# A slot of its own for the fourth weight chunk of an output projection

## The chip, the cores and the metric

The kernel runs on one core of a Trainium2 chip. The metric is the device time of one execution, in microseconds (us); lower is better. The engines are called PE (TensorE, matmuls; PEld are its weight loads), DVE (VectorE), ACT (ScalarE), POOL (GpSimd) and SP (SyncE, which here only issues DMAs). Each engine works off its own list of instructions in order.

## What is computed

One layer of an encoder over 1024 prompt tokens and 256 sample tokens, width 1024, all in float32. Shortened:

```
n  = rmsnorm(h);  z = n @ w_in
oa = diff_attention(...)          # 4 heads, two softmax maps each
ob = gqa_attention(...)           # 8 query heads, 2 kv heads
h  = h + concat(oa, ob) @ w_out   # the output projection
h  = h + relu(rmsnorm(h) @ w_ff1)**2 @ w_ff2
h  = h + sigmoid(rmsnorm(h) @ w_gate) * (p @ w_proj)
y  = rmsnorm(h)
```

## The kernel before

Float32 products are made from three matmuls of split operands: a high part (the value rounded to a shorter format, by an ACT copy) and a low part (the value less the high part, by a subtraction), multiplied as high x high, high x low and low x high. So every weight is loaded raw, split by ACT and POOL or DVE, and then used.

The stages are: the input projections, attention, the feed-forward layer, the gate. Attention is laid out in rounds; each round has a few score matmuls, softmax pieces, transposes (`tr`), splits of the transposed weights (`ph`, `pl`) and value matmuls (`av`). Between the pieces of a round the program weaves other matmul work from one generator, `side_work`: first the rest of the query and key projections (`qk_rest`, tiles `psa`, whose results `zl` are scaled by the row `R`), then the output projection in two passes, each over four of the eight 128-row chunks of `w_out`. The first pass takes chunks 0, 1, 4 and 5 (`first` is true), the second 2, 3, 6 and 7. A pass goes over the ten 128-token tiles in the order `TORD`; for each it loads the attention result `mt` (512 KB, from DRAM, where attention stores it as `md`), makes two groups of 12 matmuls into `pso` (4 chunks x 3 products, 512 columns each), and adds them to the residual row `h_sb` on DVE (L973). In the first pass each `mt` load is followed on SP by the load of a token row from `x` (L929).

The memory on the right-hand side of a partition is first used by the pools of the projections (`xh` and `xl`, the split inputs, `R`, the weight and result buffers). `open_out_proj` (L874) closes them and opens, over the same bytes, seven slots H0 to H6 of 10,240 bytes and nine slots W0 to W8 of 4,096. Two further slots, Q0 and Q1, lie on the left. A slot holds one tile at a time: whoever takes it next waits until all readers of the tile before are done.

What the change touches is the loading of the first pass's weights in `out_proj`, L931 to L939:

- chunk 0 is loaded into Q1 by `qk_rest` (L869), long before;
- chunks 1 and 4 are loaded by `opw_dma` without a tag: their halves land in the unused last quarters of the residual tiles H1 to H4 (`h_sb<-in_w_out` in the profile);
- the fourth, chunk 5, is loaded into Q1 again (L938), after the split of chunk 0; `wor<-in_w_out` in the profile is Q1's loads, chunk 0's and chunk 5's;
- `opw_split` (L905) splits each chunk in two halves: two ACT copies (L914) and two POOL subtractions (L915). `Y` sets how many rounds pass between the splits.

`load_mt` (L922) gives the `mt` tiles W6, W7 and W8 in turn, so the first `mt` lies in W6, the second in W7 and the third in W8.

The code gives each instruction its dependencies; the order of each engine's list, SP's among them, is drawn up when the program is built, from when each instruction is expected to be ready. It is therefore not the order of the code: chunk 0's load, in the code at the end of `qk_rest`, is issued at 213.1 us, and chunk 5's, in the code ahead of the first `mt` load, behind the third.

Of the kernel before, what the change touches and what calls it, by code (L numbers as in the profile page):

```python
# [41 lines left out]
def f(ap):  # L42
    return ap.bitcast(F32)
# [3 lines left out]
def encoder_kernel(ctx: ExitStack, tc: tile.TileContext, x, xT, pT, w_in, w_out, w_ff1, w_ff2, w_gate, w_proj,  # L47
# [168 lines left out]
    def slot(tag, shape, dt, name):  # L216
        return slot_pool[tag].tile(shape, dt, tag=tag, name=name, bufs=1)
# [63 lines left out]
    def mm_gen(ps, pairs, step=6):  # L281
        n = len(pairs)
        for i, (a, b) in enumerate(pairs):
            PE.matmul(ps, a, b, start=i == 0, stop=i == n - 1)  # L284
            if i % step == step - 1:
                yield step * ps.free_size() * 0.422
        if n % step:
            yield (n % step) * ps.free_size() * 0.422
# [583 lines left out]
    op_state = {}  # L872
# [11 lines left out]
    def h_row(t):  # L884
        j, half = divmod(TORD.index(t), 2)
        return op_state["h"][j][:, half * D:half * D + D]
# [6 lines left out]
    def opw_dma(ch, tag=None):  # L893
        if tag:
            t = slot(tag, [P, D], F32, "wor")
            raws = [t[:, i * 512:i * 512 + 512] for i in range(2)]
        else:

            n = next(raw_n) % 2
            raws = [op_state["h"][2 * n + i + RO][:, 2 * D:] for i in range(2)]  # L900
        for i in range(2):
            dma(raws[i], w_out[ch * P:(ch + 1) * P, i * 512:i * 512 + 512])
        return raws

    def opw_split(raws):  # L905
        n = next(ow_n) % 5
        if n < 2:
            w = slot32(f"H{5 + n}", [P, 2, D], F32R, "ow")
            a, b = w[:, 0], w[:, 1]
        else:  # L910
            a, b = (slot(f"W{2 * n - 4 + i}", [P, D], F32R, "ow")[:] for i in range(2))
        for i, raw in enumerate(raws):
            c = slice(i * 512, i * 512 + 512)
            S.activation(a[:, c], raw, AF.Copy)  # L914
            G.tensor_tensor(b[:, c], raw, f(a[:, c]), op=ALU.subtract)  # L915
        return a, b

    def out_proj(chs, ws, ahead, banks, first):

        mts = {}  # L920

        def load_mt(it):  # L922
            t = TORD[it]
            mt = mts[it] = slot(("W6", "W7", "W8")[it % 3 if first or it < 6 else it % 2], [P, 4, 2, P], F32R, "mt")
            d = dma(f(mt[:]), md[0 if first else 1][:, :, :, t * P:(t + 1) * P])
            if first:
                with tc.issue_after(d.ins):
                    for t_ in TORD[it + XA if it else 0:it + 1 + XA]:
                        dma(h_row(t_), x[t_ * P:(t_ + 1) * P])  # L929

        if first:  # L931
            raws = [op_state.pop("w0"), opw_dma(chs[1]), opw_dma(chs[2])]
            for n in range(4):
                for _ in range(Y[n > 0]):
                    yield 0.0
                ws.append(opw_split(raws.pop(0)))
                if n == 0:
                    raws.append(opw_dma(chs[3], "Q1"))  # L938
                    load_mt(0)  # L939
        else:  # L940
            raws = []
            for n, ch in enumerate(chs):
                if n >= len(ws):
                    raws.append(opw_dma(ch))
                    if len(raws) == 2:
                        yield 0.0
                        yield 0.0
                        ws.append(opw_split(raws.pop(0)))
            while raws:
                ws.append(opw_split(raws.pop(0)))  # L950
        nb = 0
        for it, t in enumerate(TORD):
            while any((ch, t // 2 * 256) not in md_done for ch in chs):
                yield 0.0
            if it not in mts:
                load_mt(it)
            mt = mts.pop(it)
            if it == 0:
                for _ in range(Y[2]):
                    yield 0.0  # L960
            for n0 in range(0, D, 512):
                ps = banks[nb % len(banks)]("pso")
                nb += 1
                pr = []
                for i in range(4):
                    mh, ml = (mt[:, i, v, :] for v in range(2))
                    a, b = (w[:, n0:n0 + 512] for w in ws[i])
                    pr += [(mh, a), (mh, b), (ml, a)]
                yield from mm_gen(ps, pr, 3)

                def evac(ps=ps, t=t, n0=n0):
                    h = h_row(t)[:, n0:n0 + 512]
                    V.tensor_tensor(h, ps, h, op=ALU.add)  # L973

                deferred.append(evac)
                yield 0.0
            if not first:
                op_done.append(t)
            if ahead and it in (2, 5):
                ahead.pop(0)()  # L980
# [4 lines left out]
    def side_work():  # L985
        yield from qk_rest()
        flush()
        open_out_proj()
        chs2 = (2, 3, 6, 7)
        ahead = []  # L990
        for ch in chs2[:2]:
            box = []
            ahead.append(lambda ch=ch: w_next.append(opw_split(opw_dma(ch))))
        yield from out_proj((0, 1, 4, 5), [], ahead, [pj], True)
        yield from out_proj(chs2, w_next, None, banks2, False)
# [884 lines left out]
```

## Time and profile before

| | |
|---|---|
| median of 3 runs | 1682.07 us (1681.45 to 1683.6) |
| profiled execution | 1681.64 us |
| its span, first to last instruction | 1679.9 us |
| mean granted TensorE clock | 0.996 |
| DMA traffic | 309.22 MB, mean 184 GB/s |
| DMA in 420 to 440 us, 440 to 460 us | 239 and 299 GB/s |

The profile is of one execution. A busy share counts the time in which an engine executes; idle time is put down to what ended it. A timeline row gives the start, the length, the engine, the line in the code, the operation, and the tile written and those read, without buffer numbers; in square brackets stands how long the engine had been idle before it and what released it. A window row gives the busy time of each engine in a stretch, then the TensorE clock granted (1.00 is full), the mean busy share of the DMA engines, and what they moved. SPq is SP's DMA queue: a row there is the issue of a transfer, whose landing is told apart. Attention ends, and the feed-forward layer begins, at some 750 us; the first output projection's matmuls begin at 444.9 us.

### The profile page before, as it was taken

To read this page: it belongs to the slowest core of one execution; us is meant where nothing else is said; L and a number is where in the kernel's file an instruction comes from. 1 tells how busy PE (TensorE), PEld (TensorE's weight loads), DVE (VectorE), ACT (ScalarE), POOL (GpSimd) and SP (SyncE) were. 2 spreads that over 40 slices of the span, in tenths; PEclk is the share of its full clock that TensorE was granted. 3 is DMA by queue.
4 is the path that set the end of the run, shared out by engine and by line. 5 is a ranking of instruction groups with operands and counts; after the bars stand their busy time and mean duration, and the time that the engine had idled before them with its cause. 6 is when DMAs were issued, how large, how long until landed. Compare 5 with 4: busy or idle time off the path is not lost. (4 is left out here: it accounts for less than half of the span.)

```text
span 1679.9 us, 27290 instructions
## 1 busy us (share of the span) xinstructions
PE 1639.0 (98%) x9777; PEld 1469.5 (87%) x9777; DVE 1202.9 (72%) x2130; ACT 879.3 (52%) x1716; POOL 664.2 (40%) x697
## 2 busy tenths in 40 slices
PE   8999999999899999999999999999999999999996
PEld 8999888888788888888999999998888888888885
DVE  7778588777788888668766666666664866855876
ACT  8543377776766667665333333333433435745533
POOL 1223455555653445333656656620433400003342
PEclk9999999999999999999999999999999999999998
DMA  9666843432954434295434443339676459980453
GB/s 330 222 221 240 246 143 112 133 109 93 271 170 129 144 87 135 95 327 192 160 118 135 148 137 132 132 137 387 233 234 196 160 187 354 337 287 13 164 205 107
DMA packets 205964, 309.22 MB, mean 184 GB/s; under 512 B 14714, under 2 KB 124932, under 8 KB 205828
## 3 DMA queue, kind: packets, MB, share of 16 engines
q1 hardware_dynamic: 203940, 301.96, 54.5%
q0 software_dynamic: 1600, 5.24, 1.1%
q8 instruction: 77, 1.26, 0.3%
q14 instruction: 59, 0.48, 0.1%
q10 hardware_dynamic: 288, 0.27, 0.0%
HBM read 200.45 MB, written 101.72 MB: 180 GB/s over the span
## 5 line engine op out<-in xcount | busy, mean ns | idle before, releaser
L671 PE MATMUL sc<-kt,qt 128*128 128x512 f32 (+1 forms) x576 | 156.4, 391 | 6.6 <-ACT p L696 4.4
L736 DVE TENSOR_TENSOR pl<-tr,ph 128x512 fp32r<-128x512 f32 x204 | 137.9, 684 | 33.7 <-ACT ph L731 32.1
L731 ACT ACTIVATE ph<-tr 128x512 fp32r<-128x512 f32 x204 | 119.8, 595 | 57.0 <-PE tr L725 50.3
L1411 DVE TENSOR_TENSOR ao<-ar,ao 128x1280 fp32r<-128x1280 f32 x56 | 96.1, 1716 | 72.0 <-ACT ao L1409 71.9
L1409 ACT ACTIVATE ao<-ar 128x1280 fp32r<-128x1280 f32 x56 | 71.0, 1270 | 128.4 <-PE f__14937 L176 31.6
L284 PE MATMUL pso<-ow,mt 128*128 128x512 f32 x480 | 120.0, 396 | 4.1 <-ACT ow L914 1.7
L725 PE MATMUL tr<-ident,p 128*128 128x128 f32 x768 | 116.0, 274 | 6.1 <-DVE pl L736 5.4
L671 PEld LDWEIGHTS sc<-kt,qt 128*128 128x128 f32 x576 | 98.9, 189 | 24.7 <-ACT p L696 5.9
L725 PEld LDWEIGHTS tr<-ident,p 128*128 128x128 f32 x768 | 91.7, 141 | 22.8 <-DVE pl L736 9.0
L284 PEld LDWEIGHTS pso<-ow,mt 128*128 128x128 f32 x480 | 87.6, 188 | 22.5 <-DVE osq L776 2.0
L1125 POOL TENSOR_SCALAR w1r<-w1r,gmlp 128x256 f32<-128x256 f32 x112 | 80.2, 733 | 67.8 <-DMA w1r<-in_w_ff 67.8
L749 PE MATMUL av<-ph,vt 128*128 128x256 f32 x544 | 101.7, 288 | 1.2 <-ACT ph L731 0.7
L710 POOL TENSOR_SCALAR p<-p,rl 128x1024 f32<-128x1024 f32 x64 | 76.1, 1190 | 50.8 <-DVE rl L708 44.5
L1198 ACT ACTIVATE w<-w1s 128x512 fp32r<-128x512 f32 x56 | 35.2, 629 | 114.7 <-POOL w1s L1205 54.9
L1696 PE MATMUL psg<-gbo,gao 128*128 128x512 f32 (+1 forms) x387 | 91.0, 385 | 0.0
L688 DVE TENSOR_REDUCE mm<-sc 128x1 f32<-128x1024 f32 (+1 forms) x80 | 84.2, 1055 | 8.9 <-PE sc L671 8.4
L749 PE MATMUL av<-pl,vt 128*128 128x256 f32 x408 | 89.1, 300 | 0.0
L1801 POOL TENSOR_TENSOR ra<-ra 128x512 f32<-128x512 f32 x5 | 7.1, 1429 | 204.9 <-DVE gao L1542 204.9
L749 PEld LDWEIGHTS av<-ph,vt 128*128 128x128 f32 x544 | 81.8, 188 | 6.5 <-ACT ph L731 0.9
L696 ACT ACTIVATE p<-sc,mm 128x1024 f32<-128x1024 f32 x64 | 71.3, 1115 | 25.4 <-DVE mm L688 16.7
L1696 PEld LDWEIGHTS psg<-gbo,gao 128*128 128x128 f32 x387 | 70.9, 188 | 14.7
L684 DVE CUSTOM_DVE_ANT_0 p<-sc,dist 128x1024 f32<-128x1024 f32 x64 | 77.6, 1218 | 7.8 <-PE sc L671 3.8
(1548 smaller groups left out, 4816.1 us busy)
## 6 DMA issues: line engine op xcount, KB each, us to landing
ar<-ad SPq DMA_DIRECT2D x56, 640.0 KB, 5.2
w2r<-in_w_ff SPq DMA_DIRECT2D x56, 512.0 KB, 5.1
qt<-qd SPq DMA_DIRECT2D x160, 128.0 KB, 2.9
ad<-q SPq DMA_DIRECT2D x64, 320.0 KB, 2.9
ad<-qs SPq DMA_DIRECT2D x48, 320.0 KB, 2.2
w1r<-in_w_ff SPq DMA_DIRECT2D x28, 512.0 KB, 4.2
md<-ml SPq DMA_DIRECT2D x40, 256.0 KB, 2.5
mt<-md SPq DMA_DIRECT2D x20, 512.0 KB, 5.9
```

What stands on the lines that cost most here:

```text
L284: PE.matmul(ps, a, b, start=i == 0, stop=i == n - 1)
L671: PE.matmul(ps[:, h0:h0 + n], shared["q"][:, cc, v, i * P:(i + 1) * P], kt[:, s0 + h0:s0 + h0 + n], start=v == 0, stop=v == 1)
L684: V.tensor_tensor_reduce(out=p[:, :sn], in0=ps[:, :sn], in1=dst_t[:, off:off + sn], scale=SLOPES[idx], scalar=3.0e38, op0=ALU.add, op1=ALU ...
L688: V.tensor_reduce(out=st["m", i][:, 0:1], in_=ps[:, :sn], axis=AX.X, op=ALU.max, negate=True)
L710: G.tensor_scalar(p[:, :sn], p[:, :sn], rl[:, 0:1], 1.0, op0=ALU.mult, op1=ALU.mult)
L725: PE.transpose(t[:, jj, i * P:(i + 1) * P], st["ws"][i][:, j * P:(j + 1) * P], ident)
L731: S.activation(ph, st["tr", j2], AF.Copy)
L736: V.tensor_tensor(pl, st["tr", j2], f(st["ph", j2][:]), op=ALU.subtract)
L749: PE.matmul(st["av"][:, :256], x_, y_, start=j2 == 0 and n == 0, stop=j2 == nj - 1 and n == len(pr) - 1)
L1125: G.tensor_scalar(raw[:, k], raw[:, k], gmlp[:, 4 * kh + k:4 * kh + k + 1], 1.0, op0=ALU.mult, op1=ALU.mult)
L1411: V.tensor_tensor(ao[:, 1], a, f(ao[:, 0]), op=ALU.subtract)
L1696: ends[:] = [PE.matmul(ps, a, w, start=n == 0, stop=n == len(pr) - 1)]
```

## The change

The fourth chunk's load moves ahead of the first split, directly behind the loads of the second and third chunk, and its raw weights land in slot W8 in place of Q1. The load in the loop goes.

```diff
         if first:
-            raws = [op_state.pop("w0"), opw_dma(chs[1]), opw_dma(chs[2])]
+            raws = [op_state.pop("w0"), opw_dma(chs[1]), opw_dma(chs[2]), opw_dma(chs[3], "W8")]
             for n in range(4):
                 for _ in range(Y[n > 0]):
                     yield 0.0
                 ws.append(opw_split(raws.pop(0)))
                 if n == 0:
-                    raws.append(opw_dma(chs[3], "Q1"))
                     load_mt(0)
```

The splits, their order and the rounds between them are as before. W8's next taker is the third `mt` tile.

## The prediction

> **What bounds the kernel now.** I read the page's first lines, then TensorE's waits around the first output projection, then the tile of the raw weights (`wor`), and last the timeline and the short windows of that stretch. On the page TensorE fills nearly the whole span; a change can only gain where it stands still or runs at a lower clock.
>
> ```profile
> span 1679.9 us, 27290 instructions
> PE 1639.0 (98%) x9777; PEld 1469.5 (87%) x9777; DVE 1202.9 (72%) x2130; ACT 879.3 (52%) x1716; POOL 664.2 (40%) x697
> ```
>
> The waits of PE between 425 and 480 us (what waited, for what: total, times, longest), and the answer for `wor`, whose landing row is the longest:
>
> ```profile
> PE sc L671 <- ACT p L696: 2.1, 2, 1.7
> PE pso L284 <- ACT ow L914: 1.7, 1, 1.7
> ...
> L914 ACT ACTIVATE ow<-wor x4: 629/638/643, 438.7 to 458.2; 128x512 fp32r<-128x512 f32 x4
> L915 POOL TENSOR_TENSOR ow<-wor,ow x4: 1272/1283/2242, 441.2 to 459.4; 128x512 fp32r<-128x512 f32 x4
> ...
> DMA to landing us min/median/max: 6.9/8.2/9.4
> ```
>
> The timeline (start, length, engine, line; in brackets the idle time before and its releaser) shows whose weights these are:
>
> ```profile
> 432.67 0.42 DVE L859 SCALAR_TENSOR_TENSOR zl<-psa,R 128x256 f32<-128x256 f32 x1
> 436.11 1.85 SPq L902 DMA_DIRECT2D h_sb<-in_w_out  x4
> 438.01 0.56 SPq L925 DMA_DIRECT2D mt<-md  x1
> 440.15 0.57 SPq L925 DMA_DIRECT2D mt<-md  x1
> 443.05 1.20 PE L671 MATMUL sc<-kt,qt 128*128 128x512 f32 x4 [1.65 <-ACT p L696]
> 443.37 1.29 POOL L915 TENSOR_TENSOR ow<-wor,ow 128x512 fp32r<-128x512 f32 x1
> 443.44 0.59 SPq L925 DMA_DIRECT2D mt<-md  x1
> 444.08 3.32 SPq L929 DMA_DIRECT2D h_sb<-in_x  x1
> 444.86 1.16 PE L284 MATMUL pso<-ow,mt 128*128 128x512 f32 x4
> 447.49 0.61 SPq L598 DMA_DIRECT2D qt<-qd  x1
> 448.20 1.16 SPq L902 DMA_DIRECT2D wor<-in_w_out  x2
> 451.27 1.30 POOL L915 TENSOR_TENSOR ow<-h_sb,ow 128x512 fp32r<-128x512 f32 x1
> 457.44 1.39 ACT L914 ACTIVATE ow<-wor 128x512 fp32r<-128x512 f32 x2 [2.99 <-DMA wor<-in_w_out]
> 458.12 0.51 PE L284 MATMUL pso<-ow,mt 128*128 128x512 f32 x1 [1.70 <-ACT ow L914]
> 458.15 2.51 POOL L915 TENSOR_TENSOR ow<-wor,ow 128x512 fp32r<-128x512 f32 x2 [2.67 <-ACT ow L914]
> 459.48 1.22 PE L284 MATMUL pso<-ow,mt 128*128 128x512 f32 x2 [0.41 <-POOL ow L915]
> ```
>
> The fourth chunk's load needs slot Q1, which POOL reads for the first chunk until 443.37 + 1.29 = 444.66. By then SP is in a row load, 444.08 to 447.40, and issues one `qt` piece first; the two halves leave from 448.20 on, 9.4 us from landing. ACT stands 2.99 us in front of the split, and because ACT works in order the softmax pieces behind it stand too: POOL is idle 2.67 us, PE 1.70 and then 0.41 us more until POOL has made the low part. Nothing else ends that wait later than the DMA.
>
> Short windows (PE busy, PEld, DVE, ACT, POOL, granted clock, DMA share, GB/s) show a second price, behind the stall:
>
> ```profile
> 442.00:444.00 2.00, 0.95 (x4) 0.81 (x5) 1.75 (x5) 2.00 (x5) 2.00 (x2) 1.00 1.10 350
> 457.00:458.00 1.00, 0.00 (x0) 0.00 (x0) 0.00 (x0) 0.56 (x1) 0.00 (x0) 1.00 1.15 261
> 458.00:459.00 1.00, 0.88 (x5) 0.63 (x5) 0.00 (x0) 0.87 (x3) 0.85 (x1) 1.00 1.18 241
> 459.00:460.00 1.00, 0.59 (x2) 0.50 (x2) 0.65 (x2) 1.00 (x4) 1.00 (x2) 0.59 1.15 257
> 460.00:461.00 1.00, 1.00 (x4) 0.74 (x3) 1.00 (x2) 0.44 (x1) 0.66 (x1) 0.50 1.05 256
> 461.00:462.00 1.00, 1.00 (x6) 0.80 (x5) 1.00 (x4) 0.41 (x1) 0.00 (x0) 0.50 1.06 377
> 462.00:463.00 1.00, 1.00 (x5) 0.88 (x5) 1.00 (x2) 0.06 (x1) 0.00 (x0) 0.71 1.01 352
> ```
>
> From 459 to 463 the clock is 0.59, 0.50, 0.50 and 0.71: 0.41 + 0.50 + 0.50 + 0.29 = 1.70 us of matmul work lost.
>
> **The change, part by part.** *The early load.* By the tiles' addresses W8 is the last 4,096 bytes of what was R, whose last reader is the DVE row at 432.67 (done 433.09). So the slot is free before the second chunk's load starts, and no new wait stands ahead of it. Two issues of 1.85/4 = 0.46 us follow the four `h_sb` pieces, at about 437.96 instead of 448.20. The last `h_sb` piece and the rate of the DMA there:
>
> ```profile
> DMA to landing us min/median/max: 5.1/5.2/5.3
> ...
> 435.00:440.00 5.00, 4.60 (x32) 3.94 (x31) 4.92 (x10) 4.63 (x10) 3.51 (x5) 1.00 1.06 281
> 440.00:445.00 5.00, 3.35 (x24) 2.81 (x23) 4.67 (x7) 4.95 (x11) 5.00 (x5) 1.00 0.93 321
> 445.00:450.00 5.00, 5.00 (x29) 4.23 (x30) 2.88 (x7) 3.97 (x10) 5.00 (x5) 1.00 1.11 349
> 450.00:455.00 5.00, 5.00 (x38) 4.65 (x37) 4.19 (x9) 3.47 (x6) 5.00 (x6) 1.00 1.09 284
> ```
>
> The piece issued at 437.5 landed at 437.5 + 5.3 = 442.8; the chunk's 524 KB at 281 to 321 GB/s take 1.6 to 1.9 us more: landed near 444.5, some 13 us earlier. The 1.70 + 0.41 = 2.11 us of PE idling go, and I let the 1.70 us of half clock go with them: together -3.8 us.
>
> *The split, moved earlier.* It keeps its two ACT pieces (2 x 0.64 us) and two POOL pieces (2 x 1.28 us), but they now queue in a stretch where POOL is busy 5.00 of 5.00 in three windows and ACT 4.95 in one. POOL's last split of the third chunk ends at 451.27 + 1.30 = 452.57; the fourth may end at 455.1 at the earliest, against 460.66 now. What is queued behind them on POOL is the scaling of `p` for later transposes. I cost that at nothing, because the 2.67 us in which POOL then stood idle cover the 2.56 us; without that cover it would be those 2.56 us, and below nothing it cannot go, since no work is removed.
>
> *`mt` and the token rows, moved back.* This is where something new is paid. The DMA is full (share 0.93 to 1.11), so 524 KB put ahead of the first `mt` delays it by about 1.6 us. Its landing is not in the trace. Its first reader, PE at 444.86, stands idle for nothing there. Behind the `h_sb` landing at 442.8 its own 524 KB (128 x 1,024 float32, as the chunk) take at least 1.6 us, so it lands near 444.4 and has about 0.4 us to spare: if PE's list stays as it is, PE stands 1.6 - 0.4 = 1.2 us; if the list puts those four matmuls behind other ready work, 0. Nothing says which; I take the middle, 0.6.
>
> *The third `mt` goes into W8 too,* so its load (443.44) and the row behind it must now wait for the fourth split. They are wanted late: the group of the third token tile is the one at 496.37.
>
> ```profile
> 496.37 3.01 PE L284 MATMUL pso<-ow,mt 128*128 128x512 f32 x12
> ```
>
> I cost it at nothing as long as SP does not stand in front of it (a rival below). The 1 MB that leaves SP's line there makes the `qt` pieces behind it earlier, not later; Q1 has no other taker in this stage.
>
> *The sum:* -2.11 - 1.70 + 0.6 = -3.2 us, from 0 to 1.2 us for `mt` -3.8 to -2.6. The profiled execution took 1681.64 us (span 1679.9 and 1.7 around it), 0.43 below the median of 1682.07; so about 1678.4 for it and **1678.9** for the median, 1678.3 to 1679.5. The gain lasts to the end if PE stays the bound: from 480 to 700 us it is busy 211.76 of 220.
>
> ```profile
> 480.00:700.00 220.00, 211.76 (x1293) 182.61 (x1294) 178.90 (x340) 151.94 (x318) 99.63 (x112) 1.00 0.38 114
> ```
>
> **A rule against one term.** The clock fell after idle pieces of 1.70 and 0.41 us with 0.9 us of work between; the 1.65 us hole that ends at 443.05 (PE busy 0.95 of 2 us) had left it at 1.00. So the length of one hole alone does not tell. The Trainium skill, "TensorE: Matmul & The Clock Gate", Part 1, has the clock halved after an idle window of about 3.4 us, on windows that run freely. Taken strictly, neither hole is long enough, the fall would not be this stall's, and the sum would be -2.11 + 0.6 = -1.5. The trace leans the other way: the fall begins right behind the stall, and in the other windows shown, from 435 to 700 us, the clock is 1.00.
>
> **The rivals.** A change of 0.2%, 3.4 us, is about what a measurement of this kernel tells from none: faster is below 1678.7, slower above 1685.4.
>
> *SP stands before the third `mt` (slower).* If SP's list keeps that load where it is, SP waits from 444.2 until the fourth split has been read out, 455.1 at the earliest; the row behind takes 3.3 and the issue 0.6, so the `qt` piece of 447.49 leaves at 459.0. It landed 9.0 us after its issue, at 456.5; on an emptier queue the page gives 2.9:
>
> ```profile
> DMA to landing us min/median/max: 9.0/9.0/9.0
> ...
> qt<-qd SPq DMA_DIRECT2D x160, 128.0 KB, 2.9
> ...
> SPq L598 <- DMA mt<-md: 2.8, 1, 2.8
> ```
>
> that is 461.9, 5.4 us late, and with a half clock (1.7) 7.1: -3.2 + 7.1 = +3.9, **1686.0**. It becomes slower than the bound once SP stands past about 454.6. Against it: SP's longest wait between 425 and 480 is 2.8 us, and its list follows readiness, not the code (the fourth load stands ahead of `load_mt(0)` in the code and was issued behind three `mt`). Chance 0.16.
>
> *The rest is put in another order.* As the list is drawn up from expected readiness, a shift here may rearrange the stage to 700 us. PE's idle time there, 220 - 211.76 = 8.2 us, bounds it both ways; half of that gives 1678.9 - 4.1 = **1674.8** to 1683.0. Chance 0.28: 0.19 faster, 0.05 within, 0.04 slower.
>
> *The stall only moves.* PE's wait for `mt` (1.2) lies close behind the hole of 1.65 us before 443.05, and the two together look like the pair that halved the clock: 1.2 + 1.7 = 2.9 are given back, 1682.07 - 0.9 = **1681.2**. Or the load isn't issued early at all: 1682.1. Chance 0.11.
>
> *The half clock isn't the stall's* and comes at that time whatever PE does before it: only the idle time goes, 1682.07 - 1.5 = **1680.6**. Chance 0.03; the fall's place right behind the stall speaks against it. The rule of the Trainium skill named above would make this the case.
>
> **How the numbers follow.** The forecast has the remaining 0.42; it counts as faster where `mt` costs under 0.45 of its 1.2 us, 0.17 of it, and 0.25 as same. Faster: 0.17 + 0.19 = 0.36. Same: 0.25 + 0.05 + 0.11 + 0.03 = 0.44. Slower: 0.16 + 0.04 = 0.20. The range goes from the reordering's 1674.8 to the slower rival's 1686.0; about 0.16 lies outside (some 0.05 below, half of the slower rival and a little of the reordering above).
>
> **What would show it.** Right: `wor` issued near 438 and landed near 445; no idle time of ACT, POOL and PE at 455 to 458 put down to it; a clock of 1.00 from 440 to 480; the span shorter by 2.6 to 3.8. For `mt`: a PE wait of up to 1.2 us at the first `pso`, or that group later in PE's list. Wrong: SP idle for several us in front of an `mt` load, with `qt` landing late; a fall of the clock elsewhere in the stage; or a gain at 460 us that is gone by 700.

## The result, and the profile after

The change makes the kernel a little slower: a median of 1684.88 us over 22 runs (1681.92 to 1688.42) against 1683.41 us over 22 runs of the kernel before on the same chips (1679.85 to 1684.82). The ratio is 1.0014, with a 95% interval of 1.0008 to 1.0020. That is 1.5 us by the medians and 2.4 us (1.3 to 3.4) by the ratio, where 3.2 us less were forecast. By the prediction's own bound of 0.2% that is "the same", and it lies in the range, but the sign is wrong.

The profiled execution took 1687.04 us, with a span of 1685.2 us. Its first page lines:

```profile
span 1685.2 us, 27293 instructions
PE 1639.6 (97%) x9777; PEld 1470.6 (87%) x9777; DVE 1201.3 (71%) x2130; ACT 879.4 (52%) x1716; POOL 667.1 (40%) x697
```

The work is the same; what has grown is time in which PE stands. Not all of the 5.3 us of span belong to the change. PE's lists of the two kernels are in the same order except between about 445 and 550 us and, for some 20 matmuls, between 690 and 711 us, and at 440 us, where the change begins, this execution is already 1.72 us late. So I compare progress instead: every matmul is given its usual spacing in the trace of before, the sums are run up in each trace, and the table says how much later (+) or earlier (-) than before's profile the same amount of work is done, set to zero at 440 us.

| at, us | 455 | 460 | 480 | 520 | 545 | 740 | 768 | 1600 |
|---|---|---|---|---|---|---|---|---|
| after | +0.52 | -2.28 | +0.31 | +0.62 | +2.07 | +2.54 | +4.56 | +3.84 |

This is the story in one row. The changed kernel gains 2.8 us between 455 and 460, where the stall was; it loses 2.6 by 480, and 1.8 more by 545, 1.45 of it behind 520. Of the 0.5 between 545 and 740 nearly all goes between 690 and 700 us. The 2 us between 740 and 768 lie where PE's lists are the same, and other profiles scatter there from -0.1 to +3.6.

The answer for `wor`, PE's and ACT's waits between 425 and 480 us (what waited, for what: total, times, longest), and SP's issues there:

```profile
who waited for it (us, times):
busy tenths in 40 slices 0000000000200000000000000000000000000000
DMA to landing us min/median/max: 5.5/6.2/6.9
```
```profile
ACT ow L914 <- DMA h_sb<-in_w_out: 4.1, 2, 3.6
...
PE tr L725 <- DVE pl L736: 1.3, 1, 1.3
...
PE av L768 <- ACT o L764: 0.9, 1, 0.9
```
```profile
437.87 1.86 SPq L902 DMA_DIRECT2D h_sb<-in_w_out  x4
439.83 0.85 SPq L902 DMA_DIRECT2D wor<-in_w_out  x2
440.72 0.68 SPq L925 DMA_DIRECT2D mt<-md  x1
...
452.94 3.66 SPq L902 DMA_DIRECT2D h_sb<-in_w_out  x4
456.87 0.56 SPq L925 DMA_DIRECT2D mt<-md  x1
```

The fourth chunk is loaded behind the second and third and lands by 439.83 + 6.9 = 446.7; nothing is listed under who waited for it. But ACT's wait for a weight has not gone: `wor` has become `h_sb<-in_w_out`, 3.6 us long. Those are the halves that leave SP at 452.94, the second pass's first chunk. The third `mt` leaves at 456.87, behind them; SP does not stand before it. Now ACT and PE at that place:

```profile
460.93 1.35 ACT L914 ACTIVATE ow<-h_sb 128x512 fp32r<-128x512 f32 x2 [3.64 <-DMA h_sb<-in_w_out]
```
```profile
459.57 3.00 PE L284 MATMUL pso<-ow,mt 128*128 128x512 f32 x12
463.45 0.70 PE L768 MATMUL av<-osq,mean_m 128*128 128x256 f32 x2 [0.88 <-ACT o L764]
463.99 0.60 PE L725 MATMUL tr<-ident,p 128*128 128x128 f32 x4
465.89 0.65 PE L725 MATMUL tr<-ident,p 128*128 128x128 f32 x4 [1.31 <-DVE pl L736]
467.03 1.21 PE L671 MATMUL sc<-kt,qt 128*128 128x512 f32 x4 [0.48 <-DVE mm L684]
```

ACT reaches that split at 460.93 - 3.64 = 457.29. Less the 1.72 us by which this execution is late that is 455.57; in before ACT reached the same split at 462.06 (its row starts at 463.17 after a wait of 1.11). So ACT stands 6.5 us earlier at that split. Part of this is the stall that is gone (a_pin, below, has before's order and is there at 460.40 - 0.44 = 459.96), the rest is the split's new place in ACT's list. Its load has moved forward by only 455.93 - (452.94 - 1.72) = 4.7 us (in before these halves leave at 455.93), and needs 8.0 us to land. PE has also put its next 12 `pso` matmuls ahead of the small `av<-osq` matmul, which starts the next softmax pieces; when they are done it waits for ACT, then for DVE, then for DVE again: 2.67 us.

The third loss is at 535 us: a hole that before's list doesn't have, and a half clock behind it (PE's row, then short windows with the granted clock behind the engines):

```profile
536.62 1.93 PE L671 MATMUL sc<-kt,qt 128*128 128x512 f32 x4 [1.84 <-ACT p L696]
```
```profile
536.00:537.00 1.00, 0.38 (x1) 0.35 (x2) 0.97 (x3) 0.81 (x3) 0.03 (x1) 0.91 0.00 0
537.00:538.00 1.00, 1.00 (x4) 0.73 (x3) 0.97 (x3) 1.00 (x3) 1.00 (x1) 0.50 0.00 0
538.00:539.00 1.00, 1.00 (x4) 0.81 (x3) 1.00 (x4) 0.65 (x2) 0.74 (x2) 0.50 0.00 0
539.00:540.00 1.00, 1.00 (x3) 0.76 (x3) 1.00 (x3) 0.07 (x1) 1.00 (x2) 0.50 0.00 1
```

The half clock of 459 to 463 is gone and has come back here.

### The profile page after: what moved, and what is told of

Same layout as the page of the kernel before. It is cut to its first block, busy times and chain, and to the rows that moved or that the text cites. A ratio compares the mean times of both kernels' runs of the same rounds, so it can differ in the third digit from the quotient of the medians.

```text
span 1685.2 us, 27293 instructions
## 1 busy us (share of the span) xinstructions
PE 1639.6 (97%) x9777; PEld 1470.6 (87%) x9777; DVE 1201.3 (71%) x2130; ACT 879.4 (52%) x1716; POOL 667.1 (40%) x697
## 4 chain that ended last, share of the span: by engine, by line
PE 80%; DVE 6%; DMA 5%; issue 3%; ACT 3%; POOL 2%; SPq 0%; POOLq 0%; DVEq 0%; ACTq 0%
PE psa L284 6%; PE sc L671 6%; PE av L749 5%; PE psg L1695 4%; PE pso L284 4%; PE tr L725 4%; PE psb L284 3%; PE psv L284 2%; PE psp L176 1%; DMA xt<-in_x 1%; DVE pl L736 1%; DMA h_sb<-in_w_out 1%; PE f__15611 L176 1%; PE f__14582 L176 1%; DVE nlo L1231 1%
```

## The experiments

After reading the profile my theory was that the early load itself does what was forecast, and that the lists rearranged around it give it back: above all the second pass's first split, which ACT now meets before its load has landed (the next-weight wait). Rivals: the third `mt` in W8 is what costs; the order of the rest costs (the hole at 535 us); or the half clock of before's profile was an accident, and there was less to gain. Each run's ratio is against before in runs on the same chip. "Lag" is the table's number, from 440 us to the time named. A label that begins with a_ has the early load, one with b_ the late load of the kernel before. The kernels ran in three blocks, each with runs of before of its own; before's medians there were 1683.71 (29 runs), 1683.11 (29, with one of 2322.34 us, which the ratios leave out) and 1683.32 us (33).

**b_copy: the kernel before again, one execution.** No edit.

> The kernel before once more, unchanged, for a second profile of the same program: how far two profiles of one program differ at 440 us, at 545 us and at the end. The two profiles at hand differ by 1.7 us at 440 us, ahead of the first changed instruction, and by 1.8 us more at 790 us, where the lists are the same; if that is scatter, a second profile of before shows steps of that size at those places.

Measured: 1685.17 us, span 1683.4; at 440 us it was 2.44 us behind before's first profile, lag to 545 us -0.40. The stall is there, but ACT 2.67 us and PE 1.38 + 0.41:

```profile
460.34 0.51 PE L284 MATMUL pso<-ow,mt 128*128 128x512 f32 x1 [1.38 <-ACT ow L914]
460.68 0.60 PE L725 MATMUL tr<-ident,p 128*128 128x128 f32 x4
461.69 0.73 PE L284 MATMUL pso<-ow,mt 128*128 128x512 f32 x2 [0.41 <-POOL ow L915]
```

The last row's two matmuls take 0.73 us, where in before's profile the row of the same two took 1.22, and the granted clock behind the stall stays at 1.00:

```profile
461.00:462.00 1.00, 0.59 (x4) 0.34 (x3) 0.45 (x1) 1.00 (x4) 1.00 (x2) 1.00 1.14 250
462.00:463.00 1.00, 1.00 (x7) 0.69 (x6) 1.00 (x2) 0.69 (x3) 0.88 (x1) 1.00 1.08 275
```

So the 1.70 us that I read off that profile don't belong to each execution.

**a_copy: the kernel after again, one execution.** No edit.

> The changed kernel once more, for a second profile. If the clock's half window at 537 us is chance (its stretches of 3.41 us lie otherwise in each execution, and the second profile of before had none at 459 us), it may be missing here or lie elsewhere, and the stretch from 440 to 545 us then takes 1 to 1.7 us less than in the first profile. If the stall at 535 us always brings it, it is there again.

Measured: 1685.36 us, span 1683.6, lag +2.60 to 545 us: the three losses are no accident of one profile. ACT waits 2.04 us for the same load, the hole at 535 has its half clock again (this execution has another at 445).

**a_hold: after, with the second pass's early splits held behind the last `ph` copy.** Only two ACT and two POOL instructions and two DMAs move; PE's and DVE's lists are those of after. `last_ph` holds the `ph` copy made last; the lines that set it are left out.

```diff
-            ahead.append(lambda ch=ch: w_next.append(opw_split(opw_dma(ch))))
+            def later(ch=ch):
+                raws = opw_dma(ch)
+                with tc.issue_after(last_ph[0].ins):
+                    w_next.append(opw_split(raws))
+            ahead.append(later)
```

> The changed kernel, with the split of the second pass's first two weight chunks held in ACT's list behind the transposed-weight copy (ph) of the round that the code names, in place of being pulled forward. PE's and DVE's lists stay exactly those of the changed kernel. Theory 'next weight': in the changed kernel ACT stands 3.64 us before that split (457.3 to 460.9), and this eats the lead of 2.8 us that PE has at 460 us. Without it the lead lasts: 2 to 3.5 us faster than before (about 1680.5 against 1683.4), and PE's idle time from 460 to 480 us falls from 3.2 us to about 1. Rival 'order': PE's rearranged list as such is short of ready work; the same list gives the same time, 1.4 us slower than before. Rival 'third mt': the third attention tile and its row come too late; no change either, 1.4 slower.

Measured: 1685.31 us (11 runs), ratio 1.0009 (1.0000 to 1.0018); no better than after by its median; the 2 to 3.5 us under before that the next-weight theory expected did not come. In its profile (1682.85 us, the fastest of the eleven) the wait for the weight is gone, and at 465 us it is 3.41 us ahead; but by 480 only 1.38. PE's waits from 470 us on and its window show why:

```profile
470.96 0.51 PE L671 MATMUL sc<-kt,qt 128*128 128x256 f32 x2 [1.00 <-ACT p L696]
...
474.94 1.21 PE L671 MATMUL sc<-kt,qt 128*128 128x512 f32 x4 [0.62 <-ACT pq L696]
...
478.06 0.73 PE L749 MATMUL av<-ph,vt 128*128 128x256 f32 x4 [0.33 <-ACT ph L731]
...
479.16 1.19 PE L671 MATMUL sc<-kt,qt 128*128 128x512 f32 x4 [0.36 <-ACT p L696]
```
```profile
470.00:480.00 10.00, 7.68 (x46) 6.30 (x47) 8.34 (x16) 6.26 (x15) 4.53 (x7) 1.00 0.68 176
```

PE has done its 12 `pso` matmuls early and has nothing left to put between the softmax pieces: the order of PE's own list loses about 2 us here even where no weight is late. And the hole at 535 is there too, this time without a half clock:

```profile
534.41 1.21 PE L671 MATMUL sc<-kt,qt 128*128 128x512 f32 x4 [1.84 <-ACT p L696]
```

**b_hold: the kernel before with the same hold.** The edit against a_hold puts the late load back:

```diff
-            raws = [op_state.pop("w0"), opw_dma(chs[1]), opw_dma(chs[2]), opw_dma(chs[3], "W8")]
+            raws = [op_state.pop("w0"), opw_dma(chs[1]), opw_dma(chs[2])]
...
+                    raws.append(opw_dma(chs[3], "Q1"))
```

> The kernel before with the same hold. There ACT stood 1.11 us before that split at 463.2, behind the larger wait of 2.99 us for the fourth chunk, which stays. Theory 'next weight': 0 to 1 us faster than before. Rival 'order': any shift of the lists may move it by 2 us to either side.

Measured: 1684.08 us, ratio 1.0001 (0.9992 to 1.0009). This hold rearranged the lists as well (PE's from 471 us on), and brought the hole at 535 us with a half clock into a kernel that loads the chunk late. So that hole comes with an order of the list, not with the early load; and both runs together show that a hold in the source isn't a clean experiment here.

**a_mtq1: after, with the first pass's third `mt` in Q1 in place of W8.**

```diff
-            mt = mts[it] = slot(("W6", "W7", "W8")[it % 3 if first or it < 6 else it % 2], [P, 4, 2, P], F32R, "mt")
+            mt = mts[it] = slot("Q1" if first and it == 2 else ("W6", "W7", "W8")[it % 3 if first or it < 6 else it % 2], [P, 4, 2, P], F32R, "mt")
```

> The changed kernel with the third attention tile (mt) in slot Q1, which the change has left free, in place of W8: its load then need not wait for the fourth split. Rival 'third mt': this takes back the 1.4 us or more, 0 to 3 faster than before. Theory 'next weight' and rival 'order': the third mt is wanted only near 496 us, so the time stays that of the changed kernel, 1 to 2 us slower than before, with ACT's wait of 3 to 4 us before the second pass's first split still there.

Measured: 1684.64 us, ratio 0.9999 (0.9989 to 1.0010). Its median is 0.2 us from after's, its ratio 0.0015 below, so the shared slot costs nothing or up to about 2.5 us; the runs can't tell. In the profile the third `mt` leaves at 454.26 us, 2.6 earlier than in after, ACT's wait for the second pass's weight is still there (3.27 us, ended at 464.62), and so are the hole at 535 and its half clock.

**a_pin, a_pinhold, b_pinhold: the lists held.** To part the load from the rearranged lists, instructions of PE, DVE, ACT and POOL from 440 us on were put in a chain of ordering edges (no semaphores), in the order that they have in the kernel before: 1,444 matmuls of PE, to about 690 us, and shorter stretches of the other three. SP's list was left free. a_pin is after with that order. In a_pinhold the second pass's first split stands, beyond that, 50 places later in ACT's list and 24 in POOL's. b_pinhold is before (late load) with a_pinhold's order.

```diff
+LISTS = {
...
+def pin_lists(nc, tc):
+    made = {}
+    for i in list(nc.cur_bb.bb.instructions):
+        made.setdefault(str(i.engine).split(".")[-1], []).append(i)
+    how = mybir.DependencyInfo(mybir.DependencyClass.NoSync, mybir.DependencyReason.DATA)
+    for engine, runs in LISTS.items():
+        row = [made[engine][r + k] for r, n in runs for k in range(n)]
+        for a, b in zip(row, row[1:]):
+            tc.add_manual_dep(b, a.name, how, reason="list order")
...
+        pin_lists(nc, tc)
```

> The early load of the change, but with the lists of ACT, DVE, POOL and PE held in the order that they have in the kernel before; only SP's list is new. Counted from the last common point ahead of the change (near 440 us). Theory 'next weight': the wait for the fourth chunk is gone and PE is 2 to 3 us ahead at 460 us, but the split of the second pass's first chunk stands at its old place in ACT's list, its data land no earlier (near 462 us), and ACT's wait of 1.1 us there grows to 3 or 4; by 480 us most of the lead is gone, and from 440 to 545 us the kernel gains 0 to 1.5 us. Rival 'order': what the changed kernel lost, it lost by its rearranged lists; with the old lists the whole lead of 2.8 us stays to 545 us, and the time is some 3 us under before's.

> As the kernel with the early load and the old lists, and the two ACT copies and two POOL subtractions of the second pass's first chunk stand 50 and 24 places later in those two lists. Theory 'next weight': with both waits for weights gone the lead of 2.8 us lasts past 480 us: 2 to 3 us less than before from 440 to 545 us, and 2 to 3 us less in all. Rival 'order': the same as without the second edit, since the lists are otherwise equal. A third way: another wait comes up, and 1 us or less is left.

> The kernel before with its own lists and its late load, and only those two copies and two subtractions later. Theory 'next weight': in before that wait is 1.1 us of ACT behind a wait of 2.99 us which stays, so 0 to 1 us is gained from 440 to 545 us. 'Order': nothing moves.

| | median, us | ratio to before | lag to 445 | to 460 | to 480 | to 545 |
|---|---|---|---|---|---|---|
| after | 1684.88 | 1.0014 (1.0008 to 1.0020) | +0.59 | -2.28 | +0.31 | +2.07 |
| a_pin | 1684.01 | 1.0001 (0.9990 to 1.0011) | +1.28 | -1.59 | -1.61 | -1.57 |
| a_pinhold | 1682.07 | 0.9994 (0.9985 to 1.0003) | +1.01 | -1.87 | -3.17 | -3.37 |
| b_pinhold | 1682.44 | 0.9990 (0.9979 to 1.0001) | -0.10 | -1.68 | -2.74 | -2.68 |

With the order of before, what is gained by 460 us is kept (a_pin: -1.59, -1.61, -1.57), there is no hole at 535, and no half clock in the stage. The next-weight theory had expected ACT's wait to grow to 3 or 4 us in a_pin. It is gone (the split at 460.40 waits for nothing), but not by ACT's order alone: SP's free list lets the next chunk's load leave from 447.87 us on, 8.5 us earlier than in before by the same count.

b_pinhold gains 1.68 us by 460 with the late load. SP's list is before's up to 464 us there, so this looks like scatter of the stall itself, which in this execution held PE for 0.78 us:

```profile
456.48 0.50 PE L284 MATMUL pso<-ow,mt 128*128 128x512 f32 x1 [0.18 <-ACT ow L914]
...
458.02 0.73 PE L284 MATMUL pso<-ow,mt 128*128 128x512 f32 x2 [0.60 <-POOL ow L915]
```

The price of putting the load ahead is plain in the two early loads, +1.28 and +1.01 us to 445. About 0.5 us of it is a longer wait of PE for ACT (2.15 us, where before has 1.65), and ACT waits there for the second chunk's load; the rest is in front of the first `mt`'s reader. First a_pin's rows, then a_pinhold's, where PE's wait is put down to `mt` itself:

```profile
441.66 0.63 ACT L914 ACTIVATE ow<-h_sb 128x512 fp32r<-128x512 f32 x1 [0.38 <-DMA h_sb<-in_w_out]
...
443.98 1.20 PE L671 MATMUL sc<-kt,qt 128*128 128x512 f32 x4 [2.15 <-ACT p L696]
...
446.58 1.17 PE L284 MATMUL pso<-ow,mt 128*128 128x512 f32 x4 [0.73 <-DVE rl L708]
```
```profile
445.73 1.16 PE L284 MATMUL pso<-ow,mt 128*128 128x512 f32 x4 [0.42 <-DMA mt<-md]
```

Two things follow. With the lists of the four engines the same to 690 us, the early load is worth nothing that the times show: a_pin against before 1.0001, a_pinhold against b_pinhold 1682.07 to 1682.44 us. And holding back the next pass's split seems worth some 1 to 2 us with either load, though each interval of those two just takes in 1. a_pinhold's interval lies wholly below after's: the rearranged lists, with the next weight's place in them, cost the changed kernel 3.4 us by the two ratios (0.8 to 5.9 from end to end). Part of that is the held split, which helps the late load too; against a_pin alone it is 2.2 us, and those two intervals overlap at their ends.

Behind 690 us the lists are not the same. In a_pin and a_pinhold four transposes stand ahead of a group of 12 `pso` matmuls there, and PE waits in front of them; in before it doesn't. This is a_pin's row:

```profile
696.52 0.63 PE L725 MATMUL tr<-ident,p 128*128 128x128 f32 x4 [0.77 <-DVE pl L736]
```

Between 690 and 700 us the lag grows by 0.5 to 0.75 us in all nine profiles whose PE list has another order there (after, a_copy, a_hold, b_hold, a_pin, a_pinhold and the three of the next block), and by nothing in b_copy, b_pinhold and a_behindhold, which have before's. It takes back the 0.7 us by which a_pinhold's profile leads b_pinhold's at 545.

**a_mix, b_mix, a_mixhold: which part of the order.** My theory at this point was the hole at 535 us alone. a_mix has the early load and after's order up to 480 us, and before's order from there, so without that hole. b_mix is the reverse: the late load, before's order up to 480, after's from there. a_mixhold is a_mix with the second pass's first split 55 and 24 places later. The edit is the same code with other lists.

> The changed kernel with its own lists up to 480 us, and from there the order that the same instructions have in before's lists. New theory 'second hole': what makes the changed kernel slower is a hole of 1.84 us that its list has at 535 us (PE waits for a softmax piece), in all five profiles with that list and in none with the old one, and the half clock of 3.41 us that follows it in four of the five. With the old order from 480 us the hole is gone, the mean granted clock over the executions rises from 0.9955 to before's 0.9966, and the time falls by 1 to 1.5 us to about before's (0 to 0.6 us above it). Rival 'next weight': ACT's wait before 461 us is still there, so the time stays 1.4 us above before's.

> The converse: the kernel before, with its late load and its lists up to 480 us, and from there the order that the changed kernel has. 'Second hole': the hole of 1.8 us at 535 us comes up here, the mean granted clock falls to about 0.9955, and the time rises by 1 to 2 us over before's, with nothing of the change made. Rival 'next weight': within 0.5 us of before's.

> The changed kernel with its own lists up to 480 us except for the split of the second pass's first chunk, which stands 55 places later in ACT's list, and with before's order from 480 us. 'Second hole' and 'next weight' together: neither the wait at 461 nor the hole at 535 is left; 1 to 2 us under before's time. 'Next weight' alone: the same. 'Second hole' alone: as without the held split, before's time.

| | median, us | ratio to before | lag to 460 | to 470 | to 480 | to 545 |
|---|---|---|---|---|---|---|
| a_mix | 1685.97 | 1.0020 (1.0009 to 1.0031) | -2.62 | +0.88 | +0.76 | +1.17 |
| b_mix | 1684.49 | 1.0006 (0.9995 to 1.0016) | -0.27 | +0.05 | -0.15 | +0.63 |
| a_mixhold | 1684.10 | 1.0006 (0.9996 to 1.0016) | -0.85 | -2.08 | -0.59 | -0.21 |

The theory fell: without the hole at 535 the kernel is as slow as after, and all of its loss up to 545 comes between 460 and 470 us, behind the wait for the next weight:

```profile
461.27 1.31 ACT L914 ACTIVATE ow<-h_sb 128x512 fp32r<-128x512 f32 x2 [4.06 <-DMA h_sb<-in_w_out]
```
```profile
463.76 0.70 PE L768 MATMUL av<-osq,mean_m 128*128 128x256 f32 x2 [1.27 <-ACT o L764]
464.29 0.60 PE L725 MATMUL tr<-ident,p 128*128 128x128 f32 x4
466.23 1.11 PE L725 MATMUL tr<-ident,p 128*128 128x128 f32 x4 [1.34 <-DVE pl L736]
```

These are after's rows again, with a half clock from 465.9 us besides. Take the wait away by moving the split (a_mixhold), and 1.9 us of the median go, 2.5 us by the means of the eleven runs each (0.3 to 4.6); in a_mixhold's profile a half clock from 446 us hides part of that gain at 460. The hole's order alone (b_mix) costs 1.2 us, which its interval doesn't tell from nothing. The granted clock sides with a price of the hole: its mean over the timed runs is 0.9959 in b_mix and 0.9955 in after, which have the hole, against 0.9965 in a_mix and 0.9968 in before of the same block. a_mix against a_pin sets the order before 480 us apart, with the early load in both: 1.0020 to 1.0001, some 3 us, though the two intervals overlap at their ends and SP's lists differ too.

**a_behindhold: a version made from all this.** Before's order, the split held back, and the fourth chunk's load still early but behind the first `mt` and its two token rows on SP, so that it doesn't delay them. The edit against b_pinhold:

```diff
-            d = dma(f(mt[:]), md[0 if first else 1][:, :, :, t * P:(t + 1) * P])
+            d = mts["d"] = dma(f(mt[:]), md[0 if first else 1][:, :, :, t * P:(t + 1) * P])
...
-                    raws.append(opw_dma(chs[3], "Q1"))
                     load_mt(0)
+                    with tc.issue_after(mts["d"].ins):
+                        raws.append(opw_dma(chs[3], "W8"))
```

> Before's lists, the held split, and the fourth chunk's early load put behind the first mt and its two rows in place of ahead of them. With the load ahead, PE waited 0.4 to 0.7 us more at the first matmuls of the projection and lost 1.0 to 1.3 us up to 446 us. If that is the price of the mt, it is gone here: 0 lost up to 446, and 3.5 to 4.5 us gained from 440 to 545 us against 3.4 with the load ahead; in all 2 to 4 us under before. If it was the ACT and POOL work and not the mt, nothing changes against the load ahead.

Measured: 1681.31 us, ratio 0.9992 (0.9983 to 1.0001): 2.0 us under before and 3.6 under after by medians. Its profile has no loss at `mt` (+0.12 to 445 us) and keeps what it gains (-2.77 at 460, -2.50 at 545). SP's rows, and ACT's split of the fourth chunk, which waits for nothing:

```profile
441.92 0.56 SPq L925 DMA_DIRECT2D mt<-md  x1
442.57 1.44 SPq L929 DMA_DIRECT2D h_sb<-in_x  x2
444.06 1.41 SPq L902 DMA_DIRECT2D wor<-in_w_out  x2
```
```profile
458.31 1.14 ACT L914 ACTIVATE ow<-wor 128x512 fp32r<-128x512 f32 x2
```

It has the lowest median found; its interval still just takes in 1, and it isn't told apart from b_pinhold (0.9990), which has the same lists (PE's throughout) and loads the chunk late.

## Why the prediction was wrong

- **The stall and its cause: right.** The load left where it was said to, landed some 13 us earlier, and no engine waits for it. PE gained 2.8 us by 460 in after and 2.9 in a_pin.
- **The removed half clock, 1.70 us: the first step that failed.** The prediction took the clock of one profile as the stall's sure price. Of the five profiles with before's order and the late load in front of this stall, two have a half clock behind it (before, b_mix) and three have none (b_copy, b_hold, b_pinhold); b_copy is all the same only 0.40 us ahead at 545. Over the timed runs the mean granted clock did not rise where the stall was taken away: 0.9963 in a_pin, 0.9970 in before of the same block, and one half window would be 0.5 x 3.41 / 1684 = 0.0010. The half clock is the stall's where it comes, but it comes only in some executions (last section), so neither the forecast nor the rival that put it down to something else has it right.
- **The idle time, 2.11 us:** 2.06 us in b_mix, 1.79 in b_copy, 1.72 in b_hold and 0.78 in b_pinhold. The profile at hand had the largest of the five.
- **The delay of `mt`, taken at 0.6 of 0 to 1.2 us: about right in size, half right in kind.** In after the first `mt`'s reader waits for nothing, the forecast's case of 0; the lag of 0.52 us to 455 comes ahead of it, where ACT waits 0.48 us for the second chunk's load. With PE's list as it was, the price is 1.28 and 1.01 us, near the 1.2 forecast for that case, but only 0.73 and 0.42 of it stand in front of `mt`. The wait through ACT was not in the sum. With b_copy's stall the sum without the half clock is -1.79 + 1.28 = -0.5 us for a_pin, which its 1.0001 (0.9990 to 1.0011) agrees with.
- **The early split at no cost: right as far as seen.** In a_pin, with the load early and the lists held, nothing is lost between 460 and 545 us.
- **"Nothing else ends that wait later than the DMA": wrong in effect, the second step that failed.** It held for the wait that was removed, but the next weight split moved up to the same place in ACT's list, 6.5 us earlier, in front of a load that left only 4.7 us earlier: ACT stood 3.64 us there and PE 2.67 us behind it. The "stall only moves" rival had the wait at `mt`, and none of the rivals had it at the next weight. Price: 1.9 us between the medians of a_mix and a_mixhold.
- **The rest in another order: this rival came, but as a loss.** Of its 0.28, 0.19 stood for faster, 0.05 for the same and 0.04 for slower. By the bound of 0.2% the result is the same, but it lies past the 1683.0 that half of PE's idle time gave. The idle time was a fair bound; that the rest should most likely go in the kernel's favour had no row behind it. The order lost about 2 us between 470 and 480 in a_hold, made the hole at 535 and lost 0.5 us behind 690. Why the lists are drawn up so is not shown; my reading is that they don't know how full the DMA is.
- **SP in front of the third `mt`: did not happen.** SP's list took it behind four other loads, and a_mtq1 shows no price that can be told from none.

What stays open is how after's 1.5 us divide between the waits of 460 to 480 us and the hole at 535. A median of 11 to 33 runs settles about 1.5 us here, and each of the two is worth about that. The scatter at 745 to 768 us, in stretches with the same list of PE, is open too; in three of the fourteen profiles (a_copy, b_mix, a_behindhold) a half clock starts there.

## What to carry to other kernels

Where a tool draws up the order of each engine's list, moving one load is a change to all lists: compare their order first, and ask of the in-order engine that was waiting which wait it meets next and whether that load has also become earlier. A load put ahead in a full DMA delays what was first there, so put it behind what the next matmul needs. Compare profiles from a common point before the change, and don't bank a fall of the clock seen in one profile.

## What the runs showed of the hardware

The half-clock stretches are all 3.41 us long and start on a grid that runs through the whole execution: in a_copy they start at 444.90, 537.07 and 765.76 us, 27.0 and 67.0 times 3.413 us apart. Whether a hole costs the clock depends on how it lies on that grid. The hole of 1.84 us at 535 us lay in one grid window in after, and the clock fell; in a_hold the same hole was cut 0.91 to 0.93 us by a border, and it did not:

```profile
535.00:536.00 1.00, 1.00 (x6) 0.83 (x5) 0.97 (x3) 1.00 (x3) 0.88 (x1) 1.00 0.00 0
536.00:537.00 1.00, 1.00 (x6) 0.84 (x5) 1.00 (x4) 0.44 (x2) 0.86 (x2) 1.00 0.00 0
```

Laid on that grid, the fourteen profiles divide by PE's idle time in one window of it (400 to 790 us): behind 1.68 us or less no half clock followed, behind 1.91 us or more one always did (11 windows). Of the two windows between, the one of before's stall (1.81 us) was followed by one, and one in after at 762 us (1.83 us) was not. In b_copy a border cut the stall, and 1.38 us lay in the window.

Between 520 and 545 us after lost 1.45 us and a_hold gained 0.12, so one such stretch costs about 1.5 us there. The Trainium skill, "TensorE: Matmul & The Clock Gate", Part 1, has the free-running window of 3413 ns, and these runs agree with it in the length and the grid. It has the clock halved after an idle window of about 3.4 us; here that is too strict, since 1.81 us of idle time within one window were enough in before.
